# Splitting the weights of three mixers during the feed-forward part before each, and loading both parts from HBM

## The chip, the cores and the metric

The kernel runs on one core of one Trainium2 chip. The metric is the device time of one execution in microseconds (us); a profiled execution also leaves a trace with the start and the duration of every instruction. The engines are TensorE (PE; its weight loads are PEld), VectorE (DVE), ScalarE (ACT), GpSimd (POOL) and SyncE (SP), which here only issues transfers (DMAs). SPq marks rows of SP's queue.

## The reference

Four blocks run one after the other over 512 tokens of 1024 features, in float32. Cut to the products, a block of the first type (twice, with 16 extra tokens in front) and one of the second type (twice) are:

```
hn = rms_norm(h);  q, k, v, xr, gate = split(hn @ w_in)            # mixer of type 1
h += concat(diff_attention(q, k, v), norm(rg_lru(xr, gate))) @ w_out
g, u = split(rms_norm(h) @ w_gu);  h += (silu(g) * u) @ w_down     # its feed-forward part

cb, cc, ch, dq, dk, dv, iq, ik, iw, cq, ck, cv = split(x @ w_in2)  # mixer of type 2
score = sum_heads(iw * relu(iq @ ik));  idx = top_k(score, 128)    # the indexer, 8 heads
y = concat(conv(cb, cc, ch), attention(dq, dk[idx], dv[idx]), band_attention(cq, ck, cv))
x = layer_norm(ALPHA x + y @ w_mix)
x = layer_norm(ALPHA x + cross_attention(x, mem))
x = layer_norm(ALPHA x + relu(x @ w_ff1)**2 @ w_ff2)               # its feed-forward part
```

## The kernel before

Features lie on partitions and tokens along the free dimension; the residual and the operands of the products stay in SBUF. A weight comes in tiles of 128 output features: 128 partitions by 8 x 128 elements, 512 KB. The function `weight` (L86 to L93) brings one in: SP issues the load into `wraw` (L88), ACT casts it to the rounded type fp32r, the high part `whi` (L90), and VectorE, in some steps of the second-type mixer GpSimd (`POOLW`), subtracts that from the raw tile, which leaves the low part `wlo` (L92). Each of the three names has three buffers, so a load can run several tiles ahead of its product. A product is accurate to nearly float32 because three matmuls stand for one (`mm3`, L95 to L98): high weight by high operand, high weight by low operand, low weight by high operand. A tile's product over 512 tokens is 8 x 3 = 24 matmuls of 512 columns; in the feed-forward part of a first-type block, in two spans, 48 of 264.

The program is straight-line code. A list scheduler orders every engine's instructions from the order in which the code makes them and from when buffers come free; on the chip every engine, SP's queue among them, works its list in order, and an instruction that waits holds up all behind it.

The order within the second-type mixer is the list `STEPS2`. It begins with `H`, the input products 2, 3 and 0 over half the tokens at a time; then `I`, the product 1; then `Q0`, the indexer's scores `i2`, `Q2`, `i1`, `i3`, `Q1`, `C0` and so on. Products 0 and 1 are the indexer's queries. Each is turned by `rope`, split into the parts `nh` and `nl` (`index_in`), and then copied within SBUF by 16 small DMAs (32 partitions each) into the layout `iq` that the scores read (L845). A score is one matmul from `iq` and `ik` into the PSUM name `sc` (L880), which ACT reads with a ReLU (L882) and VectorE adds up (L884). A product `Q` is copied into `dq` by four DMAs (L908, L909).

In the trace the stages are: mixer 1 of the first type to about 260 us, its feed-forward part to 664, the second such mixer to 895 and its feed-forward part to 1243; the first mixer of the second type to 1480, cross attention to 1655, feed-forward to 2050; the second such mixer to 2260, cross attention to 2450, feed-forward to the end.

Of the kernel before, what the change touches and what calls it, by code (L numbers as in the profile page):

```python
# [25 lines left out]
# columns of the first block's packed per-feature parameters  # L26
G_MIX, G_FFN, QG, KG, SUB, CW, CB, BRG, BIG, LRU, RECG, LAM = 0, 8, 16, 17, 18, 19, 35, 39, 43, 47, 51, 55
N_PAR1 = 59
# columns of the packed shape constants
# [5 lines left out]
# columns of the second block's packed per-feature parameters  # L35
# [11 lines left out]
def both_blocks(ctx: ExitStack, tc: tile.TileContext, xT, cst, par1, w1in, w1out, w1gu, w1dn, wgate,  # L47
# [4 lines left out]
    res = ctx.enter_context(tc.tile_pool(name="res", bufs=1))  # L52
    psum = ctx.enter_context(tc.tile_pool(name="psum", bufs=1, space=bass.MemoryType.PSUM))
    EARLY = 4  # tiles of features that the norms' first centre is taken from
# [7 lines left out]
    # ---- residual (features on partitions) and constants  # L62
# [4 lines left out]
    # the operand of most products: 8 tiles in two parts each  # L67
# [14 lines left out]
    # ---- building blocks  # L82
    def f(ap):
        return ap.bitcast(F32)

    def weight(src, kt=8, eng=None):  # L86
        raw = wpool.tile([128, 8, 128], F32, name="wraw", bufs=3)
        nc.sync.dma_start(raw[:, :kt], src)  # L88
        hi = wpool.tile([128, 8, 128], F32R, name="whi", bufs=3)
        nc.scalar.copy(hi[:, :kt], raw[:, :kt])  # L90
        lo = wpool.tile([128, 8, 128], F32R, name="wlo", bufs=3)
        (eng or nc.vector).tensor_sub(lo[:, :kt], raw[:, :kt], f(hi[:, :kt]))  # L92
        return hi, lo  # L93
# [12 lines left out]
    def share(part):  # L106
        """who has the extra bank in a part of the program"""
        nonlocal extra
        extra = EXTRA[part]
# [18 lines left out]
    def rsqrt(pool, v, rows, n, between=()):  # L128
        """1/sqrt: y from half the exponent, then y (1 + a polynomial of v y^2 - 1) to the last bit"""
# [23 lines left out]
    def rnorm(pool, xs, a, b, rhs, n, eps):  # L153
        """1/sqrt(the sums of xs over the partitions, as rhs groups them, / n + eps), on every partition of a group"""
# [36 lines left out]
    def tables():  # L191
        """rope tables of the given positions"""
# [27 lines left out]
    # ================= first block  # L220
    WOUT = ((0, 4), (4, 8))  # what the mixer's output product sums over, group by group
    # weights of the second block's mixer whose low parts GpSimd makes
    POOLW = (1, 0, 1, 0, 1, 0, 1)
    # tiles of the output product over half the tokens at a time, at its end and its start
    MIXTAIL = 3
    MIXHEAD = 0
    # steps whose weights are scaled by VectorE
    BYDVE = ('A010', 'A201', 'A211')
    # the first input products of the second block's mixer
    HEAD = (2, 3, 0)  # L230
    # pairs of tiles that a norm writes as one
    MERGED = (2, 4)
    # the order of the tiles of queries for the choice of keys
    TOPK = (2, 3, 1)
    # the order of the second block's mixer: H I Q input products, i scores of the indexer, p a part of the choice of
    # keys, d attention to the chosen ones, C and A attention in chunks (pair, head, group of rows), v convolution
    STEPS2 = ('H', 'I', 'Q0', 'i2', 'Q2', 'i1', 'i3', 'Q1', 'C0', 'd0', 'A000', 'A001', 'C1', 'A011', 'A100', 'A010', 'A101', 'p', 'A110', 'A111', 'C2', 'v0', 'p', 'd3', 'p', 'p', 'A201', 'p', 'd2', 'v1', 'A200', 'p', 'd1', 'A211', 'p', 'A210')
    # the order of the first block's mixer: r recurrent branch, k q v of a head pair, a attention (pair, group of rows),
    # g gates, R their norm, w output product
# [3 lines left out]
    for l in range(2):  # L243
# [4 lines left out]
        with ExitStack() as lay:  # L248
# [7 lines left out]
            def prep(gain, a, b):  # L256
                """h times the gain, in two parts; the rows' scale comes after the product"""
# [32 lines left out]
            # lambda  # L290
# [9 lines left out]
            # q gain with the scores' scale, subln gain with 1 - lam_init, half the gates' biases  # L300
# [4 lines left out]
            # c = 8 log_sigmoid(L) = 8 (min(L, 0) - log1p(exp(-|L|)))  # L305
# [4 lines left out]
            # log1p(e) = 2 atanh(e / (2 + e)), e / (2 + e) <= 1/3  # L310
# [14 lines left out]
            with ExitStack() as mixer:  # L325
# [14 lines left out]
                def recurrent(i):  # L340
# [20 lines left out]
                    # sigmoid(z) = (1 + tanh(z / 2)) / 2  # L361
# [10 lines left out]
                    # y = c r; expm1(y) = tanh(y / 2) (exp(y) + 1); expm1(2 y) = expm1(y) (expm1(y) + 2)  # L372
# [16 lines left out]
                def rows(m, gain, spans, dst):  # L389
                    """queries or keys: normalized, turned, stacked in parts"""  # L390
# [33 lines left out]
                def values(hd):  # L424
                    # v, brought to tokens on partitions
# [18 lines left out]
                def attend1(hd, grp):  # L444
# [9 lines left out]
                    # the keys of the last tile are masked for the rows before it  # L454
# [3 lines left out]
                    for i in tiles:  # L458
# [36 lines left out]
                        # to keys on partitions  # L495
# [13 lines left out]
                    for j in range(kts):  # L509
                        # the first 16 rows see the first tile of keys only  # L510
# [13 lines left out]
                def gate(hd):  # L524
                    """the gate of the recurrent branch; its norm's scale comes after the product"""
# [45 lines left out]
            with ExitStack() as ffn:  # L571
# [6 lines left out]
                f0 = 0  # L578
                for nf in (8, 7, 7):
# [4 lines left out]
                    for i in range(nf):  # L584
                        wg_ = weight(w1gu[l, 2 * (f0 + i)])
# [13 lines left out]
                    for m in range(8):  # L599
                        w = weight(w1dn[l, m, :, f0:f0 + nf], nf)  # L600
                        for p, a, b in proj(w, ys, late):
                            nc.vector.tensor_add(h[m][:, a:b], h[m][:, a:b], p)  # L602
                    f0 += nf

    # ================= second block
# [24 lines left out]
    def phase(nm, w, xs, evac, head=0, tail=0, close=None):  # L630
        """products over nm tiles of 128 features; the first and the last few go over half the tokens at a time"""
# [6 lines left out]
    with blk2:  # L638
# [4 lines left out]
        def rope(p, a, b, kinds):  # L643
            """the first and the last 64 partitions turned by the tables of their kinds"""
# [14 lines left out]
        class Norm:  # L659
            """ALPHA x + the products, normalized over the features, half the tokens at a time  # L660

            The first tiles' mean goes out of all of them first, so that their squares need not wait for the last ones;
# [560 lines left out]
```

## Time and profile before

| | us |
|---|---|
| three runs | 2867.89, 2868.2, 2871.68 (median 2868.2) |
| the profiled execution, span of its instructions | 2861.2 |
| what lies around the span, by the median | 7.0 |
| PE busy | 2781.5 (97%) |
| DVE, ACT, POOL busy | 1736.3, 1227.4, 367.0 |
| the 16 DMA engines' mean share | 33%, 97 GB/s |

TensorE is busy nearly the whole span at the full clock, so what can be won or lost is its idle time: 2861.2 - 2781.5 = 79.7 us in all. Matmuls are pipelined and their ends are modelled, so in a window a gap shows as the starts of two matmuls lying further apart than the usual 0.233 us for 512 columns.

### The profile page before, as it was taken

How to read it: one execution, taken by the hardware profiler on the slowest of the kernel's cores; microseconds unless marked ns; L12 is line 12 of the kernel's file. 1: busy time of each engine (PE TensorE's matmuls, PEld its weight loads, DVE VectorE, ACT ScalarE, POOL GpSimd, SP SyncE). 2: the span in 40 equal slices, each digit the busy share in tenths (PEclk: the TensorE clock that was granted, in tenths of full speed). 3: DMA queues.
4: the chain of work that ended last, by engine and by line, in shares of the span. 5: the costliest groups of instructions: out<-in, count | busy, mean ns of one | idle time of the engine just before them, and what ended most of it. 6: DMA issues, size and time to landing. Idle time of an engine off the chain costs nothing.

```text
span 2861.2 us, 42993 instructions
## 1 busy us (share of the span) xinstructions
PE 2781.5 (97%) x16548; PEld 2422.5 (85%) x16548; DVE 1736.3 (61%) x3534; ACT 1227.4 (43%) x2174; POOL 367.0 (13%) x403
## 2 busy tenths in 40 slices
PE   8989999999999999999999999999999999999998
PEld 7989999999887888887889888888877898888887
DVE  7887434457888434458977573333789875633335
ACT  6665222235665222235665442332445754433323
POOL 0011000000110000002220031111322110311112
PEclk9999999999999999999999999999999999999999
DMA  4332332332333333336324123333264242233331
GB/s 146 89 79 85 90 89 85 94 89 92 99 85 100 95 92 94 94 95 166 112 82 140 59 81 97 96 96 96 70 155 132 75 136 72 60 106 95 96 96 64
DMA packets 96491, 277.18 MB, mean 97 GB/s; under 512 B 13344, under 2 KB 20000, under 8 KB 96288
## 3 DMA queue, kind: packets, MB, share of 16 engines
q1 hardware_dynamic: 96288, 274.45, 32.7%
q8 instruction: 131, 2.15, 0.3%
q14 instruction: 72, 0.59, 0.1%
HBM read 241.82 MB, written 2.10 MB: 85 GB/s over the span
## 4 chain that ended last, share of the span: by engine, by line
PE 87%; DVE 8%; issue 2%; ACT 2%; POOL 1%; DMA 1%; SPq 0%; ACTq 0%; DVEq 0%; POOLq 0%
PE mm L97 25%; PE mm L98 25%; PE mm L96 25%; PE av L96 1%; PE av L97 1%; PE av L98 1%; PE av L161 1%; DVE wlo L92 1%; PE bc L827 1%; PE av L712 1%; PE tr L827 1%; DVE sq L402 1%; PE bc L176 0%; PE sc L96 0%; PE sc L833 0%
## 5 line engine op out<-in xcount | busy, mean ns | idle before, releaser
L96 PE MATMUL mm<-xh_all,whi 128*128 128x512 f32 (+2 forms) x2752 | 926.0, 338 | 12.4 <-ACT xh_all L260 6.8
L97 PE MATMUL mm<-xl_all,whi 128*128 128x512 f32 (+2 forms) x2752 | 930.3, 339 | 1.4 <-DVE xl_all L745 0.8
L98 PE MATMUL mm<-xh_all,wlo 128*128 128x512 f32 (+2 forms) x2752 | 925.9, 337 | 0.0
L90 ACT CAST whi<-wraw 128x1024 fp32r<-128x1024 f32 (+2 forms) x460 | 465.4, 1013 | 1017.7 <-PE mm L97 823.9
L92 DVE TENSOR_TENSOR wlo<-wraw,whi 128x1024 fp32r<-128x1024 f32 (+2 forms) x437 | 540.7, 1238 | 233.7 <-ACT whi L90 231.7
L96 PEld LDWEIGHTS mm<-xh_all,whi 128*128 128x128 f32 x2752 | 518.8, 189 | 66.6 <-ACT xh_all L260 6.8
L97 PEld LDWEIGHTS mm<-xl_all,whi 128*128 128x128 f32 x2752 | 519.8, 189 | 54.5 <-DVE xl_all L745 1.8
L98 PEld LDWEIGHTS mm<-xh_all,wlo 128*128 128x128 f32 x2752 | 521.0, 189 | 49.8
L1106 POOL TENSOR_TENSOR r<-r 128x512 f32<-128x512 f32 (+1 forms) x70 | 101.9, 1456 | 531.6 <-ACT r L1105 531.6
L97 PE MATMUL mm<-yl,whi 128*128 128x264 f32 (+1 forms) x528 | 169.9, 322 | 0.1
L98 PE MATMUL mm<-yh,wlo 128*128 128x264 f32 (+1 forms) x528 | 169.5, 322 | 0.0
L96 PE MATMUL mm<-yh,whi 128*128 128x264 f32 (+1 forms) x528 | 168.5, 320 | 0.0
L673 DVE TENSOR_TENSOR hall<-hall,mm 128x512 f32<-128x512 f32 (+1 forms) x82 | 46.6, 568 | 145.9 <-PE mm L98 145.9
L593 DVE TENSOR_TENSOR su<-mm,rbc 128x264 f32<-128x264 f32 (+1 forms) x66 | 34.3, 519 | 139.8 <-PE mm L98 139.8
L602 DVE TENSOR_TENSOR hall<-hall,mm 128x264 f32<-128x264 f32 (+1 forms) x72 | 37.1, 515 | 120.6 <-PE mm L98 120.6
L97 PEld LDWEIGHTS mm<-yl,whi 128*128 128x128 f32 x528 | 99.2, 188 | 8.8 <-DVE yl L122 0.6
L96 PEld LDWEIGHTS mm<-yh,whi 128*128 128x128 f32 x528 | 99.0, 188 | 7.6
L98 PEld LDWEIGHTS mm<-yh,wlo 128*128 128x128 f32 x528 | 99.2, 188 | 7.3
L588 DVE TENSOR_TENSOR sg<-mm,rbc 128x264 f32<-128x264 f32 (+1 forms) x66 | 34.0, 517 | 103.2 <-PE mm L98 101.6
L671 DVE SCALAR_TENSOR_TENSOR hall<-hall,mm 128x512 f32<-128x512 f32 x32 | 22.0, 687 | 66.9 <-PE mm L98 66.8
L692 POOL TENSOR_TENSOR accq<-accq,nsq 128x512 f32<-128x512 f32 (+1 forms) x48 | 57.9, 1205 | 25.4 <-ACT nsq L690 24.0
L432 POOL MEMSET vh<- 128x128 f32 x8 | 1.6, 205 | 463.6 <-PE mm L98 414.8
(672 smaller groups left out, 5446.3 us busy)
## 6 DMA issues: line engine op xcount, KB each, us to landing
wraw<-w2f SPq DMA_DIRECT2D x128, 512.0 KB, 3.7
wraw<-w1gu SPq DMA_DIRECT2D x88, 512.0 KB, 3.6
wraw<-w2in SPq DMA_DIRECT2D x44, 512.0 KB, 3.9
wraw<-w1in SPq DMA_DIRECT2D x40, 512.0 KB, 3.7
wraw<-w2mkv SPq DMA_DIRECT2D x32, 512.0 KB, 3.8
wraw<-w1dn SPq DMA_DIRECT2D x32, 448.0 KB, 3.3
wraw<-w1out SPq DMA_DIRECT2D x32, 256.0 KB, 2.7
wraw<-w1dn SPq DMA_DIRECT2D x16, 512.0 KB, 3.5
```

The source lines that it names most:

```text
L90: nc.scalar.copy(hi[:, :kt], raw[:, :kt])
L92: (eng or nc.vector).tensor_sub(lo[:, :kt], raw[:, :kt], f(hi[:, :kt]))
L96: nc.tensor.matmul(ps, wh, xh, start=first, stop=False)
L97: nc.tensor.matmul(ps, wh, xl, start=False, stop=False)
L98: nc.tensor.matmul(ps, wl, xh, start=False, stop=last)
L588: nc.vector.tensor_mul(sg[:, a:b], p, r2[:, a:b])
L593: nc.vector.tensor_mul(su[:, a:b], p, r2[:, a:b])
L602: nc.vector.tensor_add(h[m][:, a:b], h[m][:, a:b], p)
L673: nc.vector.tensor_add(X(m, a, b), X(m, a, b), p)
L692: nc.gpsimd.tensor_add(self.accq[:, a:b], self.accq[:, a:b], sq[:, a:b])
L827: nc.tensor.transpose(ps[:, 128 * j:128 * j + 128], p[:, 128 * j:128 * j + 128], ident)
L1106: nc.gpsimd.tensor_mul(r[:, a:b], r[:, a:b], r[:, a:b])
```

## The change

A class `Ahead` walks a list of weight tiles during a feed-forward part. Each call of `step` first stores the two parts of the tile before into tiles in HBM (SP issues both), then loads the next tile into `araw`, casts it on ACT into `ahi` and subtracts on GpSimd into `alo` (two buffers of each). `weight` asks whether its tile has been made in advance; if so it issues two loads of 512 KB, straight into `whi` and `wlo`, and no cast, no subtraction and no `wraw` is used. `POOLW` no longer says anything for such tiles.

The lists: in the first feed-forward part 20 tiles of the second mixer's input product and 16 half tiles of its output product; in the second, 22 + 8 tiles of the first second-type mixer; in the third, 22 + 8 of the second one. The very first mixer, the cross attentions and all feed-forward weights go the old way.

Comments went out too, so line numbers differ: `weight` is at L122 to L135 of the changed code, its made loads at L127, its raw load at L131, the `Ahead` load at L110 and its stores at L100; `iq` is L900 there, `dq` L963 and L964, a score L935.

```diff
+    made = {}
+
+    def place(src):
+        return src.tensor.name, src.offset
+
+    class Ahead:
+
+        def __init__(self, pool, todo):
+            self.pool, self.todo, self.kept = pool, iter(todo), None
+
+        def store(self):
+            if self.kept:
+                for d, t in self.kept:
+                    nc.sync.dma_start(d, f(t))
+            self.kept = None
+
+        def step(self):
+            self.store()
+            src, kt = next(self.todo, (None, 0))
+            if src is None:
+                return
+            raw, hi, lo = (self.pool.tile([128, 8, 128], dt, name=n, bufs=2)[:, :kt]
+                           for n, dt in (("araw", F32), ("ahi", F32R), ("alo", F32R)))
+            nc.sync.dma_start(raw, src)
+            nc.scalar.copy(hi, raw)
+            nc.gpsimd.tensor_sub(lo, raw, f(hi))
+            n, at = place(src)
+            to = [dram.tile([128, kt, 128], F32, name=f"{n}{p}{at}") for p in "hl"]
+            self.kept = list(zip(to, (hi, lo)))
+            made[n, at] = to
+
+        def finish(self):
+            while self.kept:
+                self.step()
+
     def weight(src, kt=8, eng=None):
+        if place(src) in made:
+            got = []
+            for d, n in zip(made[place(src)], ("whi", "wlo")):
+                t = wpool.tile([128, 8, 128], F32R, name=n, bufs=3)
+                nc.sync.dma_start(f(t[:, :kt]), d)
+                got.append(t)
+            return got
         raw = wpool.tile([128, 8, 128], F32, name="wraw", bufs=3)
...
+                if l == 0:
+                    ahead = Ahead(ff, [(w1in[1, m], 8) for m in W1ORDER]
+                                  + [(w1out[1, m, :, k0:k1], k1 - k0) for k0, k1 in WOUT for m in range(8)])
+                else:
+                    ahead = Ahead(ff, [(w2in[0, m], 8) for m in W2ORDER] + [(w2mix[0, m], 8) for m in range(8)])
...
                     for i in range(nf):
+                        ahead.step()
                         wg_ = weight(w1gu[l, 2 * (f0 + i)])
...
                     for m in range(8):
+                        if m % 2:
+                            ahead.step()
                         w = weight(w1dn[l, m, :, f0:f0 + nf], nf)
...
+                ahead = Ahead(ff, [] if l else [(w2in[1, m], 8) for m in W2ORDER] + [(w2mix[1, m], 8) for m in range(8)])
...
                     def up(m, p, a, b):
+                        if m % 2:
+                            ahead.step()
...
+                    def down(m, p, a, b):
+                        if m % 2 == 0 and part < 3:
+                            ahead.step()
+                        ln.add(m, p, a, b, part == 0, part == 3)
```

SP's list at the start of the first feed-forward part, before (its weights `w1gu` and `w1dn` stand alone there):

```order
40 L411 DMA k_2207<-nl 64x528 x2
41 L88 DMA wraw<-w1out 128x512 x11
42 L88 DMA wraw<-w1gu 128x1024 x16
43 L88 DMA wraw<-w1dn 128x1024 x8
44 L88 DMA wraw<-w1gu 128x1024 x14
45 L88 DMA wraw<-w1dn 128x896 x8
```

and in the middle of that part with the change (`araw` is the load of a tile to be split, `w1inh_...` and `w1inl_...` are its two parts in HBM):

```order
69 L110 DMA araw<-w1in 128x1024 x2
70 L131 DMA wraw<-w1gu 128x1024
71 L100 DMA w1inh_4592<-ahi 128x1024
72 L100 DMA w1inl_4593<-alo 128x1024
73 L100 DMA w1inh_4784<-ahi 128x1024
74 L131 DMA wraw<-w1gu 128x1024
75 L100 DMA w1inl_4785<-alo 128x1024
76 L110 DMA araw<-w1in 128x1024 x2
77 L131 DMA wraw<-w1gu 128x1024
```

About one tile is now loaded, split and stored for each of the part's own weights.

SP's list in the first second-type mixer, before, from the input weights to the third that stands among the small copies (lines of `ik`, `dk` and further `iq` rows left out):

```order
100 L88 DMA wraw<-w2in 128x1024 x6
...
104 L88 DMA wraw<-w2in 128x1024
...
107 L88 DMA wraw<-w2in 128x1024
...
110 L845 DMA iq<-nh 32x512
111 L845 DMA iq<-nl 32x512
...
126 L88 DMA wraw<-w2in 128x1024
127 L845 DMA iq<-nh 32x512 x2
128 L845 DMA iq<-nl 32x512 x2
...
141 L88 DMA wraw<-w2in 128x1024
142 L908 DMA dq<-nh 64x512 x2
143 L909 DMA dq<-nl 64x512 x2
144 L88 DMA wraw<-w2in 128x1024
```

and the same place with the change:

```order
422 L127 DMA whi<-w2inh_11241 128x1024
...
424 L127 DMA wlo<-w2inl_11242 128x1024
425 L127 DMA whi<-w2inh_11323 128x1024
426 L900 DMA iq<-nh 32x512
427 L900 DMA iq<-nl 32x512
...
442 L127 DMA wlo<-w2inl_11324 128x1024
443 L900 DMA iq<-nh 32x512 x2
444 L900 DMA iq<-nl 32x512 x2
...
457 L127 DMA whi<-w2inh_11405 128x1024
458 L963 DMA dq<-nh 64x512 x2
459 L964 DMA dq<-nl 64x512 x2
460 L127 DMA wlo<-w2inl_11406 128x1024
```

The loads of `whi` and `wlo` stand at the places of the raw loads. Of the loads here the pair 11241, 11242 is Q0's weight, 11323 and 11324 are Q2's, 11405 and 11406 Q1's: Q2's low part has 16 `iq` copies ahead of it, Q1's high part all 32, and Q1's low part the four `dq` copies as well. In the list before, 6 + 1 + 1 = 8 input weights stand ahead of the first `iq` copy; with the change it is five pairs and the high part of the sixth.

SP's list at the same place in the second such mixer, with the change:

```order
...
691 L127 DMA whi<-w2inh_18657 128x1024
...
694 L900 DMA iq<-nh 32x512
695 L900 DMA iq<-nl 32x512
...
710 L127 DMA wlo<-w2inl_18658 128x1024
711 L900 DMA iq<-nh 32x512 x2
712 L900 DMA iq<-nl 32x512 x2
...
725 L127 DMA whi<-w2inh_18703 128x1024
726 L963 DMA dq<-nh 64x512 x2
727 L964 DMA dq<-nl 64x512 x2
728 L127 DMA wlo<-w2inl_18704 128x1024
```

Here everything stands one weight earlier: 18657 and 18658 are Q0's parts, 18703 and 18704 Q2's; Q0's low part has 16 `iq` copies ahead of it, Q2's high part all 32.

## Rows read from the trace of the kernel before

**Rows 1.** The page, busy time (part 1) and the chain that ended last (part 4).

```profile
PE 2781.5 (97%) x16548; PEld 2422.5 (85%) x16548; DVE 1736.3 (61%) x3534; ACT 1227.4 (43%) x2174; POOL 367.0 (13%) x403
...
PE 87%; DVE 8%; issue 2%; ACT 2%; POOL 1%; DMA 1%; SPq 0%; ACTq 0%; DVEq 0%; POOLq 0%
```

**Rows 2.** Busy time of each engine by stage; (x) is instructions, last columns as headed.

```profile
core 0: us, PE busy (x) PEld busy (x) DVE busy (x) ACT busy (x) POOL busy (x), PEclk, DMA share, GB/s
...
255.00:640.00 385.00, 384.90 (x3155) 384.09 (x3156) 184.84 (x316) 113.66 (x143) 0.00 (x0) 1.00 0.31 93
640.00:895.00 255.00, 246.12 (x1657) 215.66 (x1656) 213.00 (x515) 150.68 (x281) 31.50 (x47) 1.00 0.33 91
895.00:1250.00 355.00, 355.00 (x1541) 288.02 (x1540) 165.68 (x210) 106.65 (x130) 0.00 (x0) 1.00 0.33 97
1250.00:1400.00 150.00, 143.71 (x749) 117.65 (x749) 123.25 (x287) 74.60 (x160) 36.69 (x45) 1.00 0.53 142
...
1990.00:2140.00 150.00, 138.21 (x749) 115.63 (x748) 108.52 (x208) 65.74 (x123) 46.90 (x43) 0.99 0.40 109
2140.00:2260.00 120.00, 117.01 (x634) 96.03 (x632) 112.29 (x342) 83.39 (x203) 19.19 (x38) 1.00 0.37 105
```

**Rows 3.** The page, DMA issues: out<-in queue count, KB each, us to landing.

```profile
wraw<-w2in SPq DMA_DIRECT2D x44, 512.0 KB, 3.9
...
wraw<-w1out SPq DMA_DIRECT2D x32, 256.0 KB, 2.7
```

**Rows 4.** Groups by line and shape: busy us and mean ns, idle before.

```profile
L90 ACT CAST whi<-wraw 128x1024 fp32r<-128x1024 f32 (+2 forms) x460 | 465.4, 1013 | 1017.7 <-PE mm L97 823.9
L92 DVE TENSOR_TENSOR wlo<-wraw,whi 128x1024 fp32r<-128x1024 f32 (+2 forms) x437 | 540.7, 1238 | 233.7 <-ACT whi L90 231.7
...
L92 POOL TENSOR_TENSOR wlo<-wraw,whi x23: 2366/2405/2651, 1300.0 to 2479.8; 128x1024 fp32r<-128x1024 f32 x23
```

**Rows 5.** Busy time in 4 to 16 us, the densest DMA.

```profile
4.00:16.00 12.00, 8.72 (x47) 8.41 (x48) 9.87 (x19) 10.91 (x19) 0.00 (x0) 1.00 0.99 379
```

**Rows 6.** Who TensorE waited for in 640:895, 1250:1400 and 1990:2140.

```profile
PE tr L500 <- DVE p L493: 3.3, 4, 1.4
...
PE sc L880 <- ACT p L882: 4.2, 4, 1.7
...
PE sc L880 <- ACT p L882: 4.7, 5, 1.7
PE bc L722 <- DVE nwy L148: 2.2, 2, 1.3
```

**Rows 7.** TensorE around the second index product, first mixer: start us, duration, line, tiles.

```profile
1286.52 0.39 PE L96 MATMUL mm<-xh_all,whi 128*128 128x512 f32 x1
...
1297.67 0.52 PE L880 MATMUL sc<-ik,iq 128*128 128x384 f32 x2
```

**Rows 8.** SP's queue in 1262:1335, same columns.

```profile
1289.53 0.56 SPq L845 DMA_DIRECT2D iq<-nh  x1
...
1299.69 0.53 SPq L88 DMA_DIRECT2D wraw<-w2in  x1
...
1313.11 0.58 SPq L88 DMA_DIRECT2D wraw<-w2in  x1
...
1318.94 0.53 SPq L88 DMA_DIRECT2D wraw<-w2in  x1
```

**Rows 9.** TensorE and then SP in the second mixer, same columns.

```profile
2077.91 0.39 PE L96 MATMUL mm<-xh_all,whi 128*128 128x512 f32 x1
...
2082.33 0.54 SPq L845 DMA_DIRECT2D iq<-nh  x1
...
2093.09 0.58 SPq L88 DMA_DIRECT2D wraw<-w2in  x1
...
2105.26 0.58 SPq L88 DMA_DIRECT2D wraw<-w2in  x1
...
2110.76 0.53 SPq L88 DMA_DIRECT2D wraw<-w2in  x1
```

More of the change, by code (lines that the diff above doesn't have):

```diff
@@ L52, in both_blocks @@
     res = ctx.enter_context(tc.tile_pool(name="res", bufs=1))
+    dram = ctx.enter_context(tc.tile_pool(name="dram", bufs=1, space=bass.MemoryType.DRAM))
     psum = ctx.enter_context(tc.tile_pool(name="psum", bufs=1, space=bass.MemoryType.PSUM))
@@ L221, in both_blocks @@
     WOUT = ((0, 4), (4, 8))
+    W1ORDER = (12, 8, 13, 4, 14, 0, 15, 5, 1, 9, 6, 2, 10, 3, 17, 11, 7, 18, 16, 19)
+    W2ORDER = (2, 3, 0, 1, 4, 6, 5, 7, 8, 9, 10, 11, 12, 13, 14, 15, 16, 17, 18, 19, 20, 21)
     POOLW = (1, 0, 1, 0, 1, 0, 1)
@@ L603, in both_blocks @@
                     f0 += nf
+                ahead.finish()
     FULL = [(0, S)]
@@ L1109, in both_blocks @@
                     phase(8, ups[part], x2, up, head=0 if part else 3)
-                    phase(8, lambda m: w2f2[l, m, :, 8 * part:8 * part + 8], ys,
-                          lambda m, p, a, b: ln.add(m, p, a, b, part == 0, part == 3),
+                    def down(m, p, a, b):
+                        if m % 2 == 0 and part < 3:
+                            ahead.step()
+                        ln.add(m, p, a, b, part == 0, part == 3)
+                    if part == 3:
+                        ahead.finish()
+                    phase(8, lambda m: w2f2[l, m, :, 8 * part:8 * part + 8], ys, down,
                           tail=3 if part == 3 else 0,
```

## The prediction

> **What bounds the kernel now.** I read the busy times and the chain of the page first [rows 1]: TensorE works in 97% of the span and is 87% of the chain that ended last; VectorE is 8% of it. So no load, cast or subtraction costs anything by its own length: it costs where TensorE waits for it, and it pays back where TensorE waited and no longer does. The table by stage says where that can be [rows 2]. In the first two feed-forward parts TensorE is busy 384.90 of 385 and 355.00 of 355 us: nothing to win there. In the mixers it idles: 255 - 246.12 = 8.9 us in the second mixer of the first type, 150 - 143.71 = 6.3 in the front of the first second-type mixer, 11.8 and 3.0 in the front and the rest of the second. VectorE, from which the change takes the subtractions, is at 213 of 255, 123 of 150 and 112 of 120 us there. Then I read whom TensorE waits for [rows 6], and for the place where the waits are, the front of the second-type mixers, SP's queue beside TensorE's starts [rows 7 to 9].
>
> **What goes, and its worth.** A made weight saves ACT a cast of about 1.05 us (1.013 mean over all shapes) and VectorE a subtraction of 1.24, or GpSimd one of 2.4 [rows 4]. Of these a mixer has 22 + 8, the first-type one 20 and 16 half ones. The casts sat idle 823.9 of 1017.7 us waiting for a matmul to free a buffer [rows 4]: weights are normally ready early, and only a subtraction that stands in VectorE's list just ahead of an instruction TensorE waits for is worth anything. The waits named are by VectorE and ACT work on activations: 3.3 us for the softmax in the first-type mixer, 4.2 and 4.7 for the ReLU of the scores, 2.2 for the norm's root [rows 6]. The subtractions lie among these, not in front of all. Bounds: nothing, and all the idle of the three mixers, 8.9 + 6.3 + 11.8 and twice 3.0 (the rest of the first second-type mixer taken like that of the second), 33 us. I take 3 in the first-type mixer (one of the two or three us-sized waits, as large as the softmax one) and 4.5 in the two others together, outside the stretches below: 7.5.
>
> **What the feed-forward parts take on.** Per tile: two stores and a load of 512 KB, one cast, one GpSimd subtraction. Cover, engine by engine, for the first part: ACT has 113.7 of 385 us busy and gets 20 x 1.05 and 16 halves, 29 more; GpSimd has none and gets 20 x 2.4 and 16 halves, 67; VectorE is untouched. The queue is the narrow one. One weight of the part is 48 matmuls; 384.9 us over 3155 of them is 0.122 each, 5.86 us a weight. The order puts about one made tile beside each weight, so SP moves 4 x 0.524 = 2.10 MB in 5.86 us, 358 GB/s, where the trace shows 379 GB/s with the DMA engines 0.99 busy [rows 5]. In SP's order the tiles go in pairs: two loads, then the four stores, which wait for the casts and for two subtractions. One such round by the rows: load 3.9 from issue, cast 1.05 and as much again for another ACT instruction ahead of it, 2 x 2.4 subtraction, the issues 0.6, some 11.4 us, against 2.24 weights x 5.86 = 13.1 us of TensorE. So it fits, with a tenth over. Behind a store that waits stand the part's own raw loads on SP's queue; TensorE has the raw and the split buffers ahead of it, 3 + 3 weights of which some four are full, 23 us, and these take up what does not fit. I cost the parts at nothing; without that cover the second rival below is the price.
>
> [...]
>
> **What is late next: the front of the second-type mixers.** A made weight needs no split, but both parts are loaded, late: a `whi` buffer comes free only when a product three tiles back is done, and there is no `wraw` stage ahead of it. In before eight weights have been issued ahead of the index copies, so Q0, Q2, Q1 and C0 fill TensorE while the scores go through ACT and VectorE. Now only five and a half are, and the others stand behind the copies at places where before had raw loads for later weights. Their times I take from before: the copies hang on the same products.
>
> First mixer. The second index product starts at 1286.52 [rows 7], the first copy is issued at 1289.53, a raw load behind 16 copies at 1299.69, one behind all 32 at 1313.11, one behind the `dq` copies at 1318.94 [rows 8]. With the change these are Q2's low, Q1's high and Q1's low part. A load of 512 KB lands 3.9 us after its issue [rows 3]; I take 3.6 for one that finds the engines idle. So Q1's low part is there at 1322.5. Undisturbed TensorE would want it after 48 + 24 + 2 matmuls of 0.233 and 11 scores of up to 0.18 (384 columns at the rate of 512 in 0.233; 48 matmuls in 11.15 us [rows 7] give that rate): 17.2 + 1.9 = 19.1 after 1286.5, some 1306. It stands still 16.5 us in total up to there (4.7 of them already for Q2's low part: 1303.3 against 1298.9). Before paid in this stretch too, 4.2 for the ReLUs and most of the window's other 2.1 us of idle time [rows 2, 6]: 5.9. Net +10.6. Behind the waiting product stand, on TensorE, the next scores, so ACT's ReLUs and VectorE's sums and top-k rounds come later as well; TensorE asks for the top-k's outcome only from the mixer's middle on (steps d3, d2, d1).
>
> Second mixer. One weight earlier in the list: Q0's low part at 2093.09 + 3.6 = 2096.7, Q2's high at 2105.26, its low at 2110.76 + 3.6 = 2114.4 [rows 9]. TensorE wants that last one after 50 matmuls and some 18 scores, 11.7 + 2.7 = 14.4 after 2077.91, 2092.3. Stand-still 22.1, against 4.7 and about 2 of smaller waits before [rows 6]: +15.4. Bounds of both together: nothing, if the scores had kept TensorE that long anyway (24 of them, each with a ReLU and a VectorE step), and 16.5 + 22.1 + 8, with the 16 scores that now are bunched behind one product, about 45.
>
> The output product of the first-type mixer: its fourth made half tile gets its buffer when attention ends and is wanted 2.1 us later; a 256 KB load takes 2.7 [rows 3] and its low part follows half a us behind: +1.5 (0 to 3). The first weights of each mixer are loaded two products ahead: nothing.
>
> Sum: -7.5 + 10.6 + 15.4 + 1.5 = +20.0. The profiled execution is 2861.2 in span and 7.0 around it, which is the median 2868.2. Forecast 2888 us; its own range is 2874 to 2906.
>
> **The rivals.** *The mixers gain and the weights come in time.* The copies are not late for TensorE, since the products between can be put off until the scores are through; then the freed ACT and VectorE time counts in full. For it: VectorE at 94% of 2140 to 2260 [rows 2]. Against it: TensorE's list is fixed, the products stand in it ahead of scores. Price: between 3 and 15 of the 33 us idle, at 7.5 the time is 2861; it decides if the loads behind 16 copies are issued 5 us sooner than in [rows 8].
>
> *The feed-forward parts starve.* If a store costs the DMA engines more than a load, a made tile with its weight takes, say, 7.0 us (300 GB/s) and not 5.86; 30 to 36 tiles lose 34 to 41, of which the buffers absorb 23; three parts lose 33 to 54 on top of the forecast: 2921 to 2942, say 2930. For it: the tenth of air above; against it: a round by the rows leaves 1.7 us.
>
> *Nothing moves.* The two places are paid for by waits that before had anyway, gains and losses cancel: 2868, with 5 either way.
>
> **How the numbers follow.** Forecast 0.57, first rival 0.20, starving 0.10, nothing 0.13. Within 0.2% (5.7 us, about what a measurement of this kernel can tell from no change) is 0.13, of the third rival; faster 0.20; slower the rest, 0.67. The range is to leave out no more than 0.2: most of the first rival's gains below 2862 and the starving case above 2906 stay outside: 2862 to 2906.
>
> **What would show it.** In the profile after, TensorE's busy share in 255:640 and 895:1250 stays full and the DMA rate there doubles to 200 GB/s or more; `wraw` casts fall from 460 by 96, to 364. In the front of the second-type mixers TensorE's matmuls on `wlo` and `whi` wait for DMA, by 10 us and more in each, with the waits of scores for the ReLU smaller; the window of the first-type mixer is shorter by 1 or 2 us. I am wrong if no wait for a `whi` or `wlo` load over 3 us shows there, or if TensorE has gaps in a feed-forward part.

## The result, and the profile after

The changed kernel takes 2947.48 us (median of 4 runs, 2944.58 to 2950.62) against 2868.05 before (4 runs): ratio 1.0276, 95% interval 1.0261 to 1.029. It is 79.4 us slower. I had said 2888, so the way was right and the size was a quarter of what came.

The page of the profile after (span 2942.8, 81.6 more than before), in the lines that answer to [rows 1, 3, 4]: busy times; groups by line with busy us, mean ns, idle before; DMA issues with us to landing.

```profile
PE 2817.6 (96%) x16548; PEld 2442.7 (83%) x16548; DVE 1732.0 (59%) x3459; ACT 1231.0 (42%) x2174; POOL 536.7 (18%) x478
...
L133 ACT CAST whi<-wraw 128x1024 fp32r<-128x1024 f32 (+2 forms) x364 | 371.4, 1021 | 685.9 <-PE mm L140 568.6
...
L112 POOL TENSOR_TENSOR alo<-araw,ahi 128x1024 fp32r<-128x1024 f32 (+1 forms) x96 | 227.4, 2378 | 437.9 <-ACT ahi L111 336.4
...
araw<-w2in SPq DMA_DIRECT2D x44, 512.0 KB, 5.8
```

TensorE runs the same 16548 matmuls and is busy 2817.6 us, 36.1 more than in [rows 1]; its idle time grew from 79.7 to 125.2 us, 45.5 more. So nearly half of the loss is matmuls that took longer, and that is the clock: the mean granted clock is 0.983 against 0.995, and 2942.8 x 0.017 - 2861.2 x 0.005 = 35.7 us. The stages answer to [rows 2]; each window is moved by the delays of the table below, so that it holds the same work as before: the first feed-forward part, the first-type mixer, the second and the third feed-forward part. The third column from the right is the granted clock.

```profile
core 0: us, PE busy (x) PEld busy (x) DVE busy (x) ACT busy (x) POOL busy (x), PEclk, DMA share, GB/s
255.50:648.80 393.30, 381.17 (x3099) 379.33 (x3100) 201.43 (x306) 138.82 (x174) 71.39 (x36) 0.99 0.59 201
655.80:913.60 257.80, 246.16 (x1645) 215.19 (x1644) 187.62 (x480) 124.53 (x248) 27.40 (x47) 0.99 0.47 147
913.60:1268.60 355.00, 347.31 (x1487) 280.85 (x1487) 189.63 (x199) 130.08 (x153) 77.10 (x30) 0.99 0.65 226
1710.50:2113.70 403.20, 389.32 (x1874) 324.83 (x1873) 192.56 (x224) 156.09 (x213) 161.53 (x91) 0.98 0.59 204
```

And the third feed-forward part before:

```profile
1660.00:2046.00 386.00, 382.43 (x1873) 320.23 (x1872) 166.25 (x224) 129.05 (x184) 81.08 (x61) 1.00 0.29 91
```

The feed-forward parts have 12.1, 7.7 and 13.9 us idle, against 0.1, nothing and 3.6 in the same windows of before, and their clock is below 1. The first-type mixer, where I had hoped for 3 us, is idle 11.6 against 8.9.

To see where the delay arises I compared the start of the same instructions, VectorE's 210 additions into the residual (`hall<-hall,mm`), in each trace with that of before. The differences in us at eight of them, named by their time in before:

| run | 254, part 1 begins | 633, ends | 893, type-1 mixer done | 1235, part 2 ends | 1481, mixer done | 2046, part 3 ends | 2271, mixer done | 2840, end |
|---|---|---|---|---|---|---|---|---|
| changed kernel | 0.5 | 15.8 | 20.6 | 33.6 | 50.5 | 67.7 | 80.8 | 81.7 |
| e1, tiles made but not used | -0.1 | 19.3 | 19.2 | 33.5 | 33.4 | 45.8 | 44.6 | 44.5 |
| e2, used but not made | 2.6 | 4.6 | 10.3 | 10.9 | 25.1 | 25.2 | 38.1 | 39.2 |
| e3, later cast | 1.2 | 10.1 | 15.1 | 23.1 | 40.6 | 48.8 | 61.3 | 61.2 |
| f1, later cast, 1/8 subtraction | 1.2 | 4.2 | 9.2 | 9.7 | 25.1 | 25.7 | 37.7 | 37.5 |
| h1, zeros in place of 7/8 of it | 1.1 | 4.2 | 7.9 | 9.0 | 23.4 | 25.4 | 37.2 | 38.1 |
| g2, VectorE subtracts, half the tiles | 0.7 | 3.2 | 8.0 | 8.5 | 9.9 | 14.4 | 15.3 | 15.1 |

The losses of the changed kernel by stage are the steps of its row: 15.3, 4.8, 13.0 in block type 1, then 16.9 in the first second-type mixer, 17.2 to the end of its feed-forward part, 13.1 in the second.

**One gap in the feed-forward part, followed back.** TensorE at 375 to 383 us (start, duration, line, tiles; in brackets the idle time before a row and what ended it):

```profile
375.14 0.28 PE L140 MATMUL mm<-yl,whi 128*128 128x264 f32 x1
375.26 0.28 PE L141 MATMUL mm<-yh,wlo 128*128 128x264 f32 x1
378.37 0.51 PE L139 MATMUL mm<-yh,whi 128*128 128x264 f32 x2 [2.83 <-ACT yh L164]
...
381.86 0.59 PE L140 MATMUL mm<-yl,whi 128*128 128x264 f32 x1 [2.73 <-DVE yl L165]
...
382.47 0.42 PE L139 MATMUL mm<-yh,whi 128*128 128x264 f32 x1
382.69 0.42 PE L140 MATMUL mm<-yl,whi 128*128 128x264 f32 x1
```

It waits 2.83 us for `yh`, an operand that ACT makes, and 2.73 for `yl`, which VectorE makes. After the second wait the starts lie 0.22 us apart (382.47, 382.69) where they lay 0.12 (375.14, 375.26). ACT's list there:

```profile
374.45 1.05 ACT L111 CAST ahi<-araw 128x1024 fp32r<-128x1024 f32 x1 [5.06 <-DMA araw<-w1in]
375.80 1.04 ACT L111 CAST ahi<-araw 128x1024 fp32r<-128x1024 f32 x1 [0.30 <-DMA araw<-w1in]
376.75 1.04 ACT L133 CAST whi<-wraw 128x1024 fp32r<-128x1024 f32 x1
377.69 0.63 ACT L164 CAST yh<-su 128x528 fp32r<-128x528 f32 x1
```

A cast of a tile made in advance stood idle 5.06 us for its load; behind it came another such cast, a weight's own and only then `yh`. VectorE and GpSimd at the same time:

```profile
377.82 1.22 DVE L135 TENSOR_TENSOR wlo<-wraw,whi 128x1024 fp32r<-128x1024 f32 x1 [3.54 <-ACT whi L133]
378.96 2.84 DVE L165 TENSOR_TENSOR yl<-su,yh 128x528 fp32r<-128x528 f32 x1
```

```profile
375.58 5.67 POOL L112 TENSOR_TENSOR alo<-araw,ahi 128x1024 fp32r<-128x1024 f32 x2 [9.87 <-ACT ahi L111]
```

`yl` took 2.84 us; it takes 0.70 on average in before. It ran while GpSimd did two subtractions, which themselves took 5.67 together. In steps of 10 us the same stretch:

```profile
370.00:380.00 10.00, 6.30 (x50) 5.87 (x48) 3.75 (x5) 3.58 (x4) 4.42 (x2) 0.95 0.79 304
380.00:390.00 10.00, 8.14 (x52) 8.14 (x53) 4.23 (x5) 2.97 (x3) 2.51 (x2) 0.71 0.78 266
390.00:400.00 10.00, 10.00 (x84) 10.00 (x84) 3.16 (x6) 2.10 (x2) 3.58 (x2) 1.00 0.97 326
```

Busy 6.30 of 10, then a clock of 0.71: the granted clock was 0.50 in 380.00 to 381.80, 0.52 in 381.80 to 386.00, where the starts lie 0.22 us apart, and 1.00 in 386.00 to 388.00 and in the next step.

**The front of the second-type mixer**, answering to [rows 7, 8]: SP's queue and TensorE (Q2's low part, Q1's high, Q1's low in that order).

```profile
1322.59 0.57 SPq L900 DMA_DIRECT2D iq<-nh  x1
...
1334.31 1.68 SPq L127 DMA_DIRECT2D wlo<-w2inl  x1
...
1347.65 0.53 SPq L127 DMA_DIRECT2D whi<-w2inh  x1
...
1351.98 0.55 SPq L127 DMA_DIRECT2D wlo<-w2inl  x1
```

```profile
1337.14 0.41 PE L935 MATMUL sc<-ik,iq 128*128 128x384 f32 x1 [3.48 <-DMA iq<-nl]
1339.02 0.79 PE L141 MATMUL mm<-xh_all,wlo 128*128 128x512 f32 x1 [1.47 <-DMA wlo<-w2inl]
```

The loads stand where I had put them: 11.7 us behind the first `iq` copy the first, 25.1 the second, 29.4 the third (10.2, 23.6, 29.4 in [rows 8]); in the second mixer within 0.7 us of [rows 9]. But TensorE's waits are not the ones that I had summed. Whom it waited for (us in total, times, longest), in the 54 us of the first mixer and then of the second that are shown further down:

```profile
PE sc L935 <- DMA iq<-nl: 3.7, 2, 3.5
...
PE mm L141 <- DMA wlo<-w2inl: 2.0, 2, 1.5
```

```profile
PE sc L935 <- DMA iq<-nl: 7.6, 4, 2.2
...
PE mm L141 <- DMA wlo<-w2inl: 1.5, 1, 1.5
```

No wait for a `whi` or `wlo` load is longer than 1.54 us. The largest waits are those of scores for the `iq` copies, and the second mixer shows why:

```profile
2142.85 0.39 PE L139 MATMUL mm<-xh_all,whi 128*128 128x512 f32 x1
...
2149.50 0.41 PE L935 MATMUL sc<-ik,iq 128*128 128x384 f32 x1 [0.46 <-DVE rt L705]
2151.98 0.41 PE L935 MATMUL sc<-ik,iq 128*128 128x384 f32 x1 [2.07 <-DMA iq<-nl]
2154.57 0.66 PE L935 MATMUL sc<-ik,iq 128*128 128x384 f32 x1 [2.18 <-DMA iq<-nl]
2157.04 0.66 PE L935 MATMUL sc<-ik,iq 128*128 128x384 f32 x1 [1.81 <-DMA iq<-nl]
2159.24 0.79 PE L141 MATMUL mm<-xh_all,wlo 128*128 128x512 f32 x1 [1.54 <-DMA wlo<-w2inl]
```

The second index product starts at 2142.85. In before the first score came 11.1 us after that start, and matmuls of products stood between the scores; here it comes 6.7 after, and four scores stand one behind the other ahead of the first matmul that needs Q0's low part. A score reads four `iq` copies, which SP issues 0.63 us apart, so the scores come 2.5 us apart. The stretch of 54 us that begins just ahead of the second index product (0.5 us in the first mixer, 0.9 in the second), first after, then before:

```profile
1319.60:1373.60 54.00, 44.25 (x159) 33.08 (x159) 33.86 (x70) 14.84 (x30) 7.34 (x8) 0.84 0.61 184
2141.94:2195.94 54.00, 41.19 (x145) 29.67 (x144) 34.89 (x78) 14.03 (x30) 7.09 (x9) 0.81 0.60 180
```

```profile
1286.00:1340.00 54.00, 48.83 (x214) 37.80 (x214) 42.18 (x71) 23.13 (x41) 15.01 (x11) 1.00 0.59 157
2077.00:2131.00 54.00, 48.31 (x212) 37.32 (x212) 43.81 (x73) 23.24 (x42) 14.98 (x11) 1.00 0.61 157
```

Idle 9.8 and 12.8 us against 5.2 and 5.7, and the clock 0.84 and 0.81 against 1.00.

### The profile page after: what moved, and what is told of

The parts are those of the page before. It is cut to its first block, busy times and chain, and to the rows that moved or that the text cites. A ratio compares the mean times of both kernels' runs of the same rounds, so it can differ in the third digit from the quotient of the medians.

```text
span 2942.8 us, 43725 instructions
## 1 busy us (share of the span) xinstructions
PE 2817.6 (96%) x16548; PEld 2442.7 (83%) x16548; DVE 1732.0 (59%) x3459; ACT 1231.0 (42%) x2174; POOL 536.7 (18%) x478
## 5 line engine op out<-in xcount | busy, mean ns | idle before, releaser
L139 PE MATMUL mm<-xh_all,whi 128*128 128x512 f32 (+2 forms) x2752 | 932.7, 340 | 14.9 <-ACT xh_all L306 7.0
L133 ACT CAST whi<-wraw 128x1024 fp32r<-128x1024 f32 (+2 forms) x364 | 371.4, 1021 | 685.9 <-PE mm L140 568.6
L135 DVE TENSOR_TENSOR wlo<-wraw,whi 128x1024 fp32r<-128x1024 f32 (+2 forms) x362 | 491.7, 1358 | 281.4 <-ACT whi L133 266.9
L112 POOL TENSOR_TENSOR alo<-araw,ahi 128x1024 fp32r<-128x1024 f32 (+1 forms) x96 | 227.4, 2378 | 437.9 <-ACT ahi L111 336.4
L111 ACT CAST ahi<-araw 128x1024 fp32r<-128x1024 f32 (+1 forms) x96 | 93.8, 978 | 184.8 <-DMA araw<-w2in 54.7
L640 DVE TENSOR_TENSOR sg<-mm,rbc 128x264 f32<-128x264 f32 (+1 forms) x66 | 33.5, 514 | 70.6 <-PE mm L141 69.1
```

The source lines that it names most:

```text
L111: nc.scalar.copy(hi, raw)
L112: nc.gpsimd.tensor_sub(lo, raw, f(hi))
L139: nc.tensor.matmul(ps, wh, xh, start=first, stop=False)
L640: nc.vector.tensor_mul(sg[:, a:b], p, r2[:, a:b])
```

## The experiments

The runs whose names begin with the same letter were taken on one chip, beside runs of the kernel before (medians 2865.41 us for e, 2864.94 for f, 2864.68 for g and 2866.25 for h). "Over before" is meant against these; the changed kernel is 79.4 us over its own.

**e1 and e2: the two halves apart.** e1 never looks into `made`; e2 makes one tile only.

```diff
-        if place(src) in made:
+        if False:                                  # e1
...
+            if made:                               # e2, in step
+                made[place(src)] = [d[:, :kt] for d in first]
+                return
```

> The tiles are split and stored in HBM during the three feed-forward parts as in the changed kernel, but every mixer loads and splits its weights the old way. Theory (the loss has two separate halves, and the feed-forward half comes from the new casts standing in ScalarE's in-order list): 35 to 45 us over the kernel before, about 2908, with TensorE gaps of 3 us and more and a granted clock below 1 in the three feed-forward parts only. Rival 1, the recorded forecast (the feed-forward parts cost nothing, all is lost in the mixers): 2868, no gaps. Rival 2 (the halves are one, delays of the feed-forward part are handed on and grow in the mixers): under 20 us over before.

> Only the first tile of the first list is split and stored; every made tile of the three mixers is then loaded, in two parts, from that one pair in HBM, so that the feed-forward parts carry nothing and the products take wrong weights. Theory: the mixers' half alone, 30 to 40 us over before, about 2903, in gaps at products on whi and wlo behind the iq copies in both second-type mixers. Rival 1, the recorded forecast: 20 over, 2888, if its sizes were right for the mixers. Rival 2 (the halves are one): under 10 us over before.

e1: 2910.4 us, ratio 1.0161 (1.0146 to 1.0176), +45.0. e2: 2903.1, ratio 1.0136 (1.0119 to 1.0153), +37.7. Together 82.7, where the change itself cost 79.4: two losses that add. The table has them in their places: e1 loses in the three feed-forward parts and nowhere else, e2 in the mixers. My recorded cost of nothing for the first half is refuted. The busy time of e1 in 255:640:

```profile
255.00:640.00 385.00, 371.22 (x3001) 369.49 (x3001) 190.12 (x267) 132.40 (x165) 70.52 (x36) 0.98 0.59 203
```

**e3, e4: casts or bytes?** e3 casts a tile one step after its load was issued. e4 stores an eighth.

```diff
-            nc.scalar.copy(hi, raw)                # e3: in the next step,
-            nc.gpsimd.tensor_sub(lo, raw, f(hi))   # by split_last
...
-                    nc.sync.dma_start(d, f(t))     # e4, c = 1
+                    nc.sync.dma_start(d[:, :c], f(t[:, :c]))
```

> As the changed kernel, but a tile is cast and subtracted one step after its load was issued, and stored one step later still: the same work and the same bytes, only the cast stands later in ScalarE's list. Theory (ScalarE's list is held up by casts that wait for araw): two thirds or more of the feed-forward loss goes, 2915 to 2925. Rival (the DMA engines are short of bandwidth or GpSimd's subtractions slow VectorE): within 8 us of the changed kernel, 2940 to 2955.

> As the changed kernel, but from the second tile on only one eighth of each part is stored (64 KB of 512), and the mixers load all made tiles from the first pair, so the outputs differ; casts, subtractions and their order around stay. Theory (the casts' place decides, the bytes only through araw landing late, 5.8 us instead of 3.9): half of the feed-forward loss goes, 2920 to 2930. Rival 1 (bandwidth decides): all of it goes, 2905. Rival 2 (bytes do not matter): 2947, unchanged.

e3: 2923.8, ratio 1.0205 (1.0189 to 1.022), 58.4 over before where the changed kernel is 79.4 over: 21 of the 45 us are gone, somewhat less than half and not the two thirds that I expected. e4: 2973.14, ratio 1.0377 (1.0362 to 1.0393), 107.7 over before: slower than the changed kernel by 28, which none of my theories had. With fewer bytes the tiles come faster (GpSimd's last subtraction of the first part starts at 423 us and not at 484), and VectorE's own took longer still, in 262:500:

```profile
L138 DVE TENSOR_TENSOR wlo<-wraw,whi 128x1024 fp32r<-128x1024 f32 x37 | 64.0, 1730 | 53.9 <-ACT whi L136 53.1 <-DMA w1outl<-alo 0.5 <-issue 0.3
```

So bandwidth is not what is short, and the starving rival's mechanism falls with it. That the denser subtractions are why e4 is slower fits this row, but no run tests it by itself.

**f1, f2: GpSimd or density?** f1 is e3 with an eighth of the subtraction. f2 loads tiles through the ring of `wraw`, half as dense.

```diff
-            nc.gpsimd.tensor_sub(lo, raw, f(hi))
+            nc.gpsimd.tensor_sub(lo[:, :1], raw[:, :1], f(hi[:, :1]))   # f1; stores hi twice
...
+            raw = wpool.tile([128, 8, 128], F32, name="wraw", bufs=3)[:, :kt]   # f2
```

> As the run with the later cast (2923.8 us, 58 over before), but GpSimd subtracts only one eighth of a tile and the second store writes the high part again, so outputs differ; casts, loads and bytes stay, at nearly the same pace. Theory (what is left of the feed-forward loss, some 22 us, is GpSimd's full subtraction slowing VectorE's own, 1.59 us instead of 1.22 there): 2900 to 2908, the mixers' 38 us and little else, and VectorE's subtraction back at about 1.25. Rival (the rest is traffic or casts): 2918 to 2925.

> As the changed kernel, but a tile to be split is loaded into the ring of wraw buffers that the part's own weights use, so that it comes in program order, about one for two weights over the whole part and not one for each over its first 60%. Theory (too dense: casts that wait for late loads and GpSimd's subtractions beside VectorE's): most of the feed-forward loss of 45 us goes, 2910 to 2920. Rival (every split tile costs the same wherever it stands): 2945, unchanged; or over 2955, if one wraw buffer less starves the part's own weights.

f1: 2903.12, ratio 1.0136 (1.0121 to 1.0151), 38.2 over before and so the same as e2, which splits one tile only: the feed-forward half is gone, with all loads, casts and bytes still there. f2: 2945.35, ratio 1.0284 (1.0267 to 1.0302): nothing won, as the rival said. The first part loses 21.5 us between 254 and 633, by the same additions. But the casts now also wait longer for loads that queue for a ring buffer, so f2 does not show what the density alone is worth; in 262:640 (us in total, times, longest):

```profile
ACT ahi L111 <- DMA wraw<-w1in: 96.6, 16, 9.6
```

**g3, h1, g1: what about GpSimd's subtraction?** g3 is the changed kernel with an eighth of it; h1 adds two writes of zeros to that, so that GpSimd is as long at work; g1 is e3 with the full subtraction on VectorE.

```diff
+            nc.gpsimd.tensor_sub(lo[:, :1], raw[:, :1], f(hi[:, :1]))   # g3, h1
+            for v in (1.0, 0.0):                                        # h1
+                nc.gpsimd.memset(f(lo), v)
...
-            nc.gpsimd.tensor_sub(lo, raw, f(hi))
+            nc.vector.tensor_sub(lo, raw, f(hi))                        # g1
```

> As the changed kernel, casts where they stood, but GpSimd subtracts one eighth of a tile and the second store writes the high part again, so outputs differ; the fourth corner beside the early cast with the full subtraction (about 2945), the late cast with it (2923.8) and the late cast with one eighth (2903.1). Theory (two separate causes that add): 2920 to 2930. Rival (the early cast hurts only because a long subtraction makes loads late): 2903 to 2910.

> As the changed kernel, in nearly the same order, but GpSimd subtracts one eighth of a tile and then writes zeros over the whole of alo twice, some 2.3 us in all, so that its work is about as long as the full subtraction (2.4 us) and the stores wait for it as long, but reads almost nothing; the low parts are zero, so outputs differ. Theory A (GpSimd's subtraction hurts because it slows VectorE's operations on two SBUF tiles, 1.22 to 1.59 us): 2905 to 2915, VectorE's subtraction back at 1.23. Theory B (it hurts because it makes the chain from load to store long, so that the next loads come late and casts wait for them in ScalarE's list): 2935 to 2950.

> As the run with the later cast (2923.8 us), with the full subtraction on VectorE and not on GpSimd; nothing is left out. Theory (the rest of the feed-forward loss is GpSimd beside VectorE, and VectorE itself has room): the mixers' 38 us and at most 5 more, 2900 to 2910. Rival (the added subtraction costs wherever it runs, since it stands in a list that TensorE's operands go through): 2915 to 2925.

g3: 2906.79, ratio 1.0144 (1.0129 to 1.016), 42.1 over before. With the casts early the full subtraction costs 37 us more than an eighth of it (79.4 and 42.1 over before); with them late 20 (58.4 and 38.2). The early cast costs 21 beside the full subtraction and 4 beside an eighth. So the two causes do not simply add, against my theory: the subtraction is the cause, and the early cast makes it worse. The rival gave the number; its reason, the length of the chain, h1 tests. h1: 2904.87, ratio 1.0137 (1.012 to 1.0154), 38.6 over before: theory A, 0.1 us below its range, and by its cause. GpSimd's two writes and its small subtraction take 0.95 + 0.95 + 0.58 = 2.5 us a full tile, as long as the full subtraction, the traffic is the same (278 GB/s in 262:500, 274 in the changed kernel), and VectorE runs at its old speed:

```profile
L114 POOL MEMSET alo<- 128x1024 f32 x40 | 38.2, 954 | 2.3
L112 POOL TENSOR_TENSOR alo<-araw,ahi 128x128 fp32r<-128x128 f32 x36 | 20.8, 577 | 145.4 <-ACT ahi L111 106.2 <-DVE nwt L182 31.5 <-DMA w1inl<-alo 7.7
```

```profile
L137 DVE TENSOR_TENSOR wlo<-wraw,whi 128x1024 fp32r<-128x1024 f32 x38 | 46.5, 1224 | 63.6 <-ACT whi L135 60.5 <-DMA araw<-w1in 3.2
...
L167 DVE TENSOR_TENSOR yl<-su,yh 128x528 fp32r<-128x528 f32 x14 | 9.9, 706 | 0.1
```

The same groups in 262:500 of the kernel before and of the changed one:

```profile
L92 DVE TENSOR_TENSOR wlo<-wraw,whi 128x1024 fp32r<-128x1024 f32 x38 | 46.5, 1223 | 13.5 <-ACT whi L90 13.5
...
L588 DVE TENSOR_TENSOR sg<-mm,rbc 128x264 f32<-128x264 f32 x30 | 12.8, 430 | 35.8 <-PE mm L98 35.8
...
L122 DVE TENSOR_TENSOR yl<-su,yh 128x528 fp32r<-128x528 f32 x14 | 9.8, 702 | 0.0
```

```profile
L135 DVE TENSOR_TENSOR wlo<-wraw,whi 128x1024 fp32r<-128x1024 f32 x38 | 60.5, 1593 | 47.4 <-ACT whi L133 46.1 <-DMA araw<-w1in 0.5 <-DMA w1inh<-ahi 0.5
L165 DVE TENSOR_TENSOR yl<-su,yh 128x528 fp32r<-128x528 f32 x13 | 14.3, 1100 | 5.4 <-ACT yh L164 5.4
L640 DVE TENSOR_TENSOR sg<-mm,rbc 128x264 f32<-128x264 f32 x28 | 11.4, 423 | 14.4 <-PE mm L141 13.9 <-ACT rbc L623 0.4
```

The subtraction of two SBUF tiles goes from 1223 to 1593 ns and `yl` from 702 to 1100; `sg`, which has one operand in PSUM, stays at 430 and 423; beside a GpSimd that mostly writes, all are back. The mean of 1593 hides two cases: of the 38 subtractions of VectorE in this window 21 ran beside one of GpSimd and took 1.90 us on average, up to 3.18, and the 17 others 1.22; in h1 the 22 beside GpSimd's work took 1.23. So here VectorE's operation on two SBUF tiles suffers (1.90 us against 1.22) and `sg` does not (423 ns, in the 8 of its 28 that ran beside a subtraction of GpSimd as in the others), and it suffers from GpSimd's subtraction (1.90) and not from its writes (1.23). Why these two kinds of GpSimd work differ is not shown.

In the third feed-forward part GpSimd was not idle before (81 of 386 us): there it squares `r`, from which ACT makes `y`. ACT's casts of `y` waited for `r` at most 1.7 us at a time before and up to 4.3 in the changed kernel, and TensorE waited 6.1 us in all for `y7h`. h1, with GpSimd as long at work, has no such wait of TensorE and loses 2.0 us from 1481 to 2046.

g1: 2906.66, ratio 1.0144 (1.0131 to 1.0158), 42.0 over before: the kernel's full work with 3.8 us more than f1. VectorE had room for it.

**f3, f4: the iq copies on GpSimd's queue**, with made weights (e2's program) and with before's.

```diff
-                                nc.sync.dma_start(f(iq[o:o + 32, 4 * m + e]), ...)
+                                nc.gpsimd.dma_start(f(iq[o:o + 32, 4 * m + e]), ...)
```

> As the run that only uses made weights (2903.1 us, 37.7 over before), but the 64 iq copies are issued from GpSimd's queue, so no weight load stands behind them on SP's. Theory (the mixers lose their 38 us because loads of made parts stand behind the iq copies): 2868 to 2880, two thirds or more of it gone. Rival 1 (three buffers and two loads a weight are too little lead anyway, wherever the copies stand): 2895 to 2905. Rival 2 (scores now late, GpSimd issues more slowly): over 2905.

> The kernel before with the 64 iq copies issued from GpSimd's queue. Theory (before has eight weights ahead of the copies, and waits for ReLUs of scores that wait for copies): within 6 us of before, perhaps 2 to 5 faster. Rival (copies bound the front of the mixer in before too): 8 to 12 us faster. If GpSimd issues more slowly than SP: up to 10 slower.

f3: 2882.88, ratio 1.0062 (1.0047 to 1.0077), 17.9 over before: 20 of e2's 37.7 us gone, a little less than the two thirds expected. f4: 2889.53, ratio 1.0089 (1.0074 to 1.0104): 24.6 slower than before, outside what I expected; GpSimd's copies land in 3.1 us and not in 2.0. So f3 is better compared with f4, whose copies are on the same queue: made weights are then 6.6 us faster than raw ones, with the copies on SP 37.7 slower. By the same additions f3 loses 6.2 and gains 0.5 us against before in the two second-type mixers, where e2 lost 14.2 and 12.9. So what the made weights lose there hangs on sharing SP's list with the copies. It does not split what the place in the queue costs from what the scheduler's other order of products and scores costs, which comes with it; that stays open.

**g2: a version with both causes taken out.** g1, and the first eleven input weights of each second-type mixer left to the old way.

```diff
-[(w2in[0, m], 8) for m in W2ORDER]
+[(w2in[0, m], 8) for m in W2ORDER[11:]]
```

> As that, and the first eleven input weights of each second-type mixer, up to the first dq copies behind the iq copies, go the old way; the other eleven, the output weights and the first-type mixer's are made in advance. Theory (only the loads behind the iq copies hurt; later ones pay): the 38 us of the mixers go except some 9 in the first-type mixer, so 2870 to 2880, or 2860 to 2868 if the rest of the mixers gains 7 as at the hand-over. Rival (three buffers with two loads each are too little lead in the whole mixer): 2890 to 2905.

2879.06, ratio 1.0053 (1.004 to 1.0066): 14.4 slower than before, 65 better than the change. The second-type mixers now cost 1.4 and 0.9 us by the table, so their loss came with the first eleven input weights. Which of these, the ones ahead of the copies or the ones among them, g2 does not split; f3, which moves the copies alone, speaks for the list that they share. The later weights pay nothing either, and some 5 are left in the first-type mixer and as much in the third feed-forward part. None of these runs beats the kernel before.

## Why the prediction was wrong, point by point

- **"I cost the parts at nothing."** This is the step that failed: 45 us by e1. I compared engine shares and queue rates and took the weights' buffers as cover. The mean rates came as said, 201 and 226 GB/s; `araw` landed in 5.8 us where I had 3.9. What I did not price was GpSimd's subtraction beside VectorE's. I had VectorE as "untouched". It was not, by h1 and f1. Nor did I ask what stands behind a waiting cast in ACT's list: not only weights, of which there is a store, but `yh` and `sg`, of which there is none. The gaps in a feed-forward part were one of my two signs of being wrong.
- **The starving rival** gave a time near the result, 2930, by a mechanism that e4 and f1 refute. A rival that lands close is not shown by that.
- **The front of the second-type mixers.** My other sign was that no wait for a `whi` or `wlo` load over 3 us would show, and it came too: the longest is 1.54 us, where I had forecast 10 us and more in each mixer. The place was right, and the loads' times within 2 us; the wait was not. I had products standing in TensorE's list ahead of the scores, waiting for their weights; in the changed kernel scores stand ahead of those products and wait for their copies, 3.7 and 7.6 us. I summed +10.6 and +15.4. From the start of the second index product to the end of the mixer the kernel loses 16.9 and 15.9. That the second number is near mine is luck: TensorE is idle 9.8 and 12.8 us there, not 16.5 and 22.1, and the term for the clock was missing. Two slips in the working are small: 1303.3 less 1298.9 is 4.4 and not 4.7, which the sum does not use, and 18 scores of 0.175 us are 3.2 and not 2.7, which would make the second term 14.9.
- **The clock.** No term of my sum had it; 36.1 of the 81.6 us are busy time that grew at a lower clock. Over the whole run 45.5 us more of idle time went with these 36.1, and I had priced gaps at their length.
- **The first-type mixer.** I had -3 + 1.5; it cost 4.8, and 5.7 in e2. The wait for the half tile's load is there, 1.1 us; the gain is not: the softmax waits are 3.9 us against 3.3. Where the rest comes from is not shown.
- **Gains.** I had taken 4.5 us outside the fronts of the two second-type mixers. From the end of the last feed-forward part to the second index product the delay falls from 67.7 to 64.9 us in the second of them, 2.8 gained; in the first it stays at 33.6 (1286.52 in [rows 7], 1320.13 with the change).
- The casts of `whi` fell to 364, and the scores' waits for the ReLU from 4.2 and 4.7 us to 2.4 and 3.0, as said.

## What to carry to other kernels

Work moved to an idle engine is not free until you have asked what that engine shares with a busy one: here GpSimd's subtraction on two SBUF tiles made VectorE's 30% longer on average, and 56% where the two ran side by side, in parts where TensorE then waited for VectorE's results (2.73 us for one `yl`). A wait in an in-order list is priced by what stands behind it (here `yh`, behind a cast that stood idle 5.06 us), not by the buffers of the thing that waits. And a gap in TensorE's work should be priced with the clock that follows it, read from the same profile: a step of 10 us after a gap had 0.71 here.

## What I had not expected of the hardware

GpSimd was slower there too: the two subtractions beside VectorE in the gap above took 5.67 us, where the median of one is 2.40. An `iq` copy issued on GpSimd took 0.50 us there and landed its 64 KB in 3.1 us (f4), against 0.59 and 2.0 on SP. And fewer bytes were slower (e4, 28 us); that the transfers had kept two engines apart is my reading of it, not shown by itself.
